# Value tiles for block A0 ahead of the dense part, and block B1's value rows summed on DVE

## The chip, the cores and the metric

The kernel runs on one core of a Trainium2 chip. The time is device microseconds of one execution; 2283.25 us is the median of three runs of the kernel before (2281.62 to 2299.92). Engines: PE multiplies matrices, DVE and POOL work on vectors, ACT on activations, and SP only issues transfers. POOL also issues the transfers whose addresses come from a list (indirect row fetches). Each engine takes its instructions in the order in which the program holds them.

## What is computed

One layer of a decoder for 512 prompt tokens and 8 sample tokens, 1024 wide, in f32. Differential attention and an mLSTM run in parallel and are merged; then comes the channel mixer, PEER, where the change lies:

```
q   = xn @ wq                         # 8 heads, two halves each
s   = q against 128 subkeys per half  # top 16 of each half, top 16 of the sums
eidx, g = 16 experts of 16384 per head, softmax of their scores
act = gelu(sum(xn * u[eidx]))         # 128 rows of peer_u per token
y   = x + sum((g * act) * v[eidx])    # 128 rows of peer_v per token
```

The prompt has two halves of 256 tokens, and each half two blocks of 128 tokens: A0 and A1 (first half), B0 and B1 (second half). The sample tokens go with the second half.

## The kernel before

For each block the scoring (`scores`, with its top-16 search) leaves 128 expert numbers and weights per token. `gather(hf, i)` then fetches, for each of the 128 columns, one row of `peer_u` per token: an indirect transfer of 512 KB (L1102, POOL) into one of six buffers of the pool `ring`, and a multiply with sum on DVE (L1108). `gelu_w` turns the sums S into weights.

The value side is computed in two ways. Blocks A0, A1 and B0 use a dense form: `w_block` spreads the weights of a block to a matrix W of 16384 experts by 128 tokens, in 32 groups of four tokens (one-hot tiles on DVE L1164, POOL L1167, DVE L1169 or L1177, ACT L145 and L1174, the products on PE L1181, copies L148), and `v_part` loads `peer_v` in 128 value tiles of 128x1024 f32 (512 KB each, L1275 on SP, five buffers) and multiplies each with the block's W (L1290, two matmuls of 512 columns per tile and block). Block B1 uses the other form, `vg_run`: 128 indirect transfers of one row of `peer_v` per expert slot of a token (L1313, POOL, twelve buffers called `vslab`) and a one-token matmul on each (L1318).

The tiles run as a ring: A0 and A1 take tiles 0 to 127 together, B0 joins at tile 100 (`JB`) and goes on alone through tiles 0 to 99; in that last piece B1's rows run beside it. W of a block occupies two slots of 64 tiles each; A0 and A1 hold two slots in each of two pools (`wr`, `wt`). W of A0 is built during the second half's scoring, W of A1 after it.

The order of the instructions on each engine is chosen by the framework's scheduler from its estimate of a time line, under the data and buffer dependencies of the program as written; on the chip it is fixed. A buffer of a pool is handed out in the program's order: whoever asks later for a buffer of `ring` waits until the one who had it before is done. `HOLD` delays the gather of a block until a step of the top-16 search.

Of the kernel before, what the change touches and what calls it, by code (L numbers as in the profile page):

```python
# [5 lines left out]
F32 = mybir.dt.float32  # L6
# [48 lines left out]
JH = 64  # L55
# [3 lines left out]
def step_kernel(  # L59
# [1051 lines left out]
    def gather(hf, i):  # L1111
        sel, todo = halves[hf]
        d, tok = sel[i], todo[i][0]
        if i == 0 and HOLD[hf] is not None:
            hb, hh = divmod(HOLD[hf], 8)
            with tc.issue_after(sel[hb]["last", hh][HE].ins):
                gather_dot(d, tok, OFF[i])
        else:
            gather_dot(d, tok, OFF[i])
        gelu_w(d["S"], d["g"], d["S"], d["top"], d["e"].bitcast(F32))  # L1120
# [63 lines left out]

    halves = []
    xx, early = project(0), None
    for hf in range(2):
# [58 lines left out]
        halves.append((scores(hf, todo, xx2), todo))  # L1246
        if hf == 0 and SV == 1:
# [24 lines left out]

    def v_part(j, use, split):
        vt = dp.tile([P, D], F32, tag="v", name="vtile", bufs=VB)
        nc.sync.dma_start(vt, v_rows[j * P:(j + 1) * P])  # L1275
        ws = [next(w[:, j - j0, :] for w, j0 in wT if j0 <= j < j0 + w.shape[1]) for _, wT, _, _ in use]
        pairs = [((w, vt),) for w in ws]
        if split:
            vh, vl = (ring.tile([P, D], F32R, tag="g", name=n) for n in ("vh", "vl"))
            wh, wl = (dp.tile([P, 2, P], F32R, tag="wh", name=n, bufs=3) for n in ("wh", "wl"))  # L1280
            copy(vh, vt)
            nc.vector.tensor_sub(vl, vt, vh.bitcast(F32))
            for b, w in enumerate(ws):
                copy(wh[:, b, :], w)
                nc.vector.tensor_sub(wl[:, b, :], w, wh[:, b, :].bitcast(F32))
            pairs = [((wh[:, b, :], vh), (wh[:, b, :], vl), (wl[:, b, :], vh)) for b in range(len(ws))]
        for (py, _, j0, j1), pp in zip(use, pairs):
            for i, (lw, rv) in enumerate(pp):
                for q in range(2):
                    nc.tensor.matmul(py[q], lw, rv[:, q * 512:(q + 1) * 512],  # L1290
                                     start=(j == j0 and i == 0), stop=(j == j1 and i == len(pp) - 1))

    def vg_prep(d, pool, wz):
        nc.gpsimd.memset(wz, 0.0)
        ef = pool.tile([P, P], F32, name="vg_ef", bufs=1)
        nc.vector.scalar_tensor_tensor(ef, d["i1"], 128.0, d["i2"], op0=ALU.mult, op1=ALU.add)
        p = pst_d()
        nc.tensor.transpose(p[:, 0:P], ef, ident)
        nc.tensor.transpose(p[:, P:2 * P], d["S"], ident)
        eT = pool.tile([P, P], I32, name="vg_eT", bufs=1)  # L1300
        nc.vector.tensor_copy(eT, p[:, 0:P])
        for j in range(4):
            copy(wz[:, j * 1024:(j + 1) * 1024:33], p[:, P + 32 * j:P + 32 * j + 32])
        return wz.rearrange("p (t c) -> p t c", c=32), eT

    def vg_run(prep, py, slots):
        wz, eT = prep
        for i in range(32):
            gts = []
            for j in range(4):  # L1310
                t = 32 * j + i
                gt = slots()
                nc.gpsimd.indirect_dma_start(out=gt, out_offset=None, in_=v_rows,  # L1313
                                             in_offset=bass.IndirectOffsetOnAxis(ap=eT[:, t:t + 1], axis=0))
                gts.append((j, t, gt))
            for q in range(2):
                for j, t, gt in gts:
                    nc.tensor.matmul(py[q][32 * j:32 * j + 32, :], wz[:, t, :], gt[:, q * 512:(q + 1) * 512],  # L1318
                                     start=(i == 0), stop=(i == 31), skip_group_check=True)
            yield  # L1320

    def v_done(tok, py):
        t = dp.tile([P, D], F32, tag="v", name="x1r", bufs=VB)
        nc.sync.dma_start(t, scr_x1[tok:tok + P])
        for q in range(2):
            nc.vector.tensor_add(t[:, q * 512:(q + 1) * 512], t[:, q * 512:(q + 1) * 512], py[q])  # L1326
        nc.sync.dma_start(y_prompt[0, tok:tok + P], t)
# [47 lines left out]
    useA = [(v_acc(0), wA0, 0, P - 1), (v_acc(1), wA1, 0, P - 1)]  # L1375
    for j in range(JH):
        v_part(j, useA, False)
    gather(1, 0)
# [3 lines left out]
    gather(1, 1)  # L1382
    wB0 = w_new(wr, wt)
    w_block(selB[0], wB0, wr, pst_d, 2)
    for j in range(JH, JB):
        v_part(j, useA, False)
    yB0 = v_acc(2)
    useB0 = (yB0, wB0, JB % P, (JB - 1) % P)
    for j in range(JB, P):
        v_part(j, useA + [useB0], False)  # L1390
    for b in range(2):
        v_done(b * P, useA[b][0])
    slab = [pool.tile([P, 8, D], F32, tag="WT", name="vslab", bufs=2) for pool in (wr, wt)]
    slot_i = [0]

    def slots():
        i = 4 + slot_i[0] % 12
        slot_i[0] += 1
        return slab[i // 8][:, i % 8, :]

    yB1 = v_acc(0)
# [46 lines left out]
```

## Time and profile before

| | |
|---|---|
| median of three runs | 2283.25 us (2281.62 to 2299.92) |
| the profiled execution | 2279.21 us, its span 2277.5 us |
| PE busy | 2098.4 us (92%) |
| DVE busy | 1403.7 us (62%) |
| POOL busy | 1327.5 us (58%) |
| ACT busy | 593.5 us (26%) |
| mean transfer rate | 303 GB/s, 690.15 MB |

The span runs from the first to the last instruction of the profiled execution. The scoring of the second half ends near 1301 us; the shared stream of A0 and A1 starts at 1351 and, with B0, holds PE to about 1930; from there B0 runs with B1's rows, and after 2194 B0 alone. A busy share is a mean over stages, so a reader takes the limit of each stage from the stretch itself.

### The profile page before, as it was taken

What the parts mean: (1) busy time and instruction counts of PE and PEld (TensorE: products, weight loads), DVE (VectorE), ACT (ScalarE), POOL (GpSimd) and SP (SyncE); (2) the same over time, 40 slices, a digit from 0 to 9 for tenths busy, and PEclk for the clock granted to TensorE, in tenths of its full rate; (3) what the DMA queues carried; (4) which work ended last, traced back from release to release, by engine and by line L of the source; (5) the groups of instructions that cost most, each with busy time, mean ns of one, the idle gap of its engine ahead of it and who ended that gap; (6) DMA issues with size and microseconds to landing.
All of it is one profiled execution on the core that took longest, in us unless ns stands there. A gap on an engine that the chain in (4) does not pass through costs nothing.

```text
span 2277.5 us, 26092 instructions
## 1 busy us (share of the span) xinstructions
PE 2098.4 (92%) x8208; PEld 1349.4 (59%) x8208; DVE 1403.7 (62%) x3382; ACT 593.5 (26%) x1615; POOL 1327.5 (58%) x1215
## 2 busy tenths in 40 slices
PE   6999899888999998998988866999999999899998
PEld 4776677777878776787766654444455544222233
DVE  1366675886799878767987989566388775000000
ACT  3334233312345323333423676000022100000000
POOL 0588773553586546667786778444278776555510
PEclk9999999989989999999998866999999999999999
DMA  5687676888799798999987147999699899999988
GB/s 161 198 269 236 229 239 229 282 297 287 243 329 324 269 321 321 337 369 313 318 311 245 43 167 248 410 409 409 252 365 355 320 403 362 410 407 409 409 332 284
DMA packets 293757, 690.15 MB, mean 303 GB/s; under 512 B 31054, under 2 KB 157066, under 8 KB 293618
## 3 DMA queue, kind: packets, MB, share of 16 engines
q0 software_dynamic: 112896, 411.09, 48.7%
q1 hardware_dynamic: 180722, 277.38, 35.1%
q8 instruction: 65, 1.06, 0.2%
q14 instruction: 74, 0.61, 0.1%
HBM read 670.19 MB, written 18.18 MB: 302 GB/s over the span
## 4 chain that ended last, share of the span: by engine, by line
PE 44%; DVE 11%; DMA 10%; issue 7%; POOL 5%; ACT 1%; DVEq 0%; POOLq 0%; ACTq 0%
PE y L1290 20%; PE ps_mm L288 9%; DMA vslab<-in_peer_v,vg_eT 6%; DVE urow L1108 3%; POOL urow L1102 3%; PE ps_mm L293 3%; PE y L1318 3%; PE ps_s L738 2%; DMA urow<-in_peer_u,k_e 1%; PE ps_w L1181 1%; POOL oh L1167 1%; PE ps_s L741 1%; DVE tk_w L975 1%; DVE ohe L1164 1%; DMA vpage<-in_cache_v,kidx 1%
## 5 line engine op out<-in xcount | busy, mean ns | idle before, releaser
L1102 POOL DMA_INDIRECT urow<-in_peer_u,k_e x512 | 632.2, 1235 | 326.9 <-DVE urow L1108 223.3
L1108 DVE SCALAR_TENSOR_TENSOR urow<-urow,xn 128x1024 f32<-128x1024 f32 x512 | 651.2, 1284 | 151.4 <-DMA urow<-in_peer_u,k_e 145.7
L1290 PE MATMUL y<-vtile,WT 128*128 128x512 f32 x1536 | 680.6, 598 | 3.0 <-DMA vtile<-in_peer_v 2.1
L1290 PEld LDWEIGHTS y<-vtile,WT 128*128 128x128 f32 x1536 | 286.6, 191 | 382.5 <-issue 377.8
L288 PE MATMUL ps_mm<-x,wch 128*128 128x264 f32 (+1 forms) x1536 | 385.9, 405 | 25.1 <-DVE sig L312 17.2
L288 PEld LDWEIGHTS ps_mm<-x,wch 128*128 128x128 f32 x1536 | 302.0, 201 | 81.5 <-DVE sig L312 20.7
L831 POOL TENSOR_TENSOR kpage<-kpage,qb 128x1024 f32<-128x1024 f32 x64 | 150.0, 2356 | 73.8 <-DMA qb<-scr_q 65.2
L288 PE MATMUL ps_mm<-hT,wch 128*128 128x256 f32 (+1 forms) x768 | 185.1, 391 | 0.7 <-DMA wch<-in_w_branch_b 0.5
L1313 POOL DMA_INDIRECT vslab<-in_peer_v,vg_eT x128 | 122.2, 955 | 106.2 <-DMA vslab<-in_peer_v,vg_eT 47.7
L1326 DVE TENSOR_TENSOR x1r<-x1r,y 128x512 f32<-128x512 f32 x8 | 5.2, 684 | 249.1 <-DMA x1r<-scr_x 238.3
L288 PEld LDWEIGHTS ps_mm<-hT,wch 128*128 128x128 f32 x768 | 144.4, 194 | 23.5 <-issue 1.3
L293 PE MATMUL ps_mm<-wch,x 128*128 128x256 f32 (+1 forms) x640 | 151.2, 388 | 0.3 <-DVE kS L690 0.3
L1318 PE MATMUL y<-vslab 128*32 128x512 f32 x512 | 138.6, 601 | 12.2 <-DMA vslab<-in_peer_v,vg_eT 12.2
L819 POOL DMA_INDIRECT vpage<-in_cache_v,kidx x64 | 79.8, 1248 | 106.6 <-DVE vacc L897 63.7
L1181 PE MATMUL ps_w<-oh,oh 128*128 128x128 f32 x512 | 88.3, 336 | 46.0 <-POOL oh L1167 29.2
L293 PEld LDWEIGHTS ps_mm<-wch,x 128*128 128x128 f32 (+1 forms) x640 | 108.3, 175 | 30.5 <-issue 2.8
L897 DVE SCALAR_TENSOR_TENSOR vacc<-vpage,aS,vacc 128x128 f32<-128x128 f32 x384 | 110.6, 359 | 19.4 <-DMA vpage<-in_cache_v,kidx 19.3
L1181 PEld LDWEIGHTS ps_w<-oh,oh 128*128 128x128 f32 x512 | 81.4, 242 | 62.3 <-POOL oh L1167 45.5
L1167 POOL TENSOR_TENSOR oh<-ohe,T_S 128x384 f32<-128x384 bf16 (+2 forms) x96 | 96.4, 1011 | 12.7 <-ACT T_S L148 5.6
L1318 PEld LDWEIGHTS y<-vslab 128*32 128x32 f32 x512 | 30.7, 109 | 112.0 <-issue 88.5
L832 DVE TENSOR_REDUCE sK<-kpage 128x16 f32<-128x1024 f32 x64 | 77.1, 1210 | 26.3 <-POOL kpage L831 26.2
L145 ACT ACTIVATE k_e<-k_top,zero 128x128 f32<-128x128 f32 x4 | 1.6, 402 | 346.0 <-DVE k_top L1126 346.0
(420 smaller groups left out, 2634.2 us busy)
## 6 DMA issues: line engine op xcount, KB each, us to landing
vtile<-in_peer_v SPq DMA_DIRECT2D x228, 512.0 KB
wch<-in_w_in SPq DMA_DIRECT2D x256, 256.0 KB
wch<-in_peer_wq SPq DMA_DIRECT2D x64, 256.0 KB
wch<-in_w_branch_a SPq DMA_DIRECT2D x32, 256.0 KB
wch<-in_w_branch_b SPq DMA_DIRECT2D x32, 256.0 KB
wch<-in_w_out SPq DMA_DIRECT2D x32, 256.0 KB
urow<-in_peer_u,k_e POOLq DMA_INDIRECT x512, 7.5
qb<-scr_q SPq DMA_DIRECT2D x8, 512.0 KB
```

What stands on the lines that cost most here:

```text
L288: nc.tensor.matmul(out, w[:, c0:c0 + m], xk[:, :n], start=(k == 0 and i == 0), stop=(k == KT - 1 and i == len(tt) - 1))
L293: nc.tensor.matmul(out, x[:, k, t0:t0 + m], ch[k // KP][:, k % KP, :n], start=(k == 0), stop=(k == KT - 1))
L819: nc.gpsimd.indirect_dma_start(out=t, out_offset=None, in_=rows, in_offset=bass.IndirectOffsetOnAxis(ap=kidx[:, b * 8 + pg:b * 8 + pg + 1] ...
L831: (nc.vector if KDV and pg % KDV == KDV - 1 else nc.gpsimd).tensor_mul(kt, kt, qb)
L897: nc.vector.scalar_tensor_tensor(acc[:, h, :], vt[:, h, :], wa, acc[:, h, :], op0=ALU.mult, op1=ALU.add)
L1102: nc.gpsimd.indirect_dma_start(out=gt, out_offset=None, in_=u_rows, in_offset=bass.IndirectOffsetOnAxis(ap=d["e"][:, k:k + 1], axis=0))
L1108: d["dot"] = nc.vector.scalar_tensor_tensor(gt, gt, 1.0, xn2, op0=ALU.mult, op1=ALU.mult, accum_out=d["S"][:, k:k + 1])
L1167: nc.gpsimd.tensor_mul(a[:, :PM], e.rearrange("p j t -> p t j")[:, :PM], sb[:, :PM])
L1181: nc.tensor.matmul(pw[:, t, :], b[:, t, :], a[:, t, :], start=True, stop=True)
L1290: nc.tensor.matmul(py[q], lw, rv[:, q * 512:(q + 1) * 512], start=(j == j0 and i == 0), stop=(j == j1 and i == len(pp) - 1))
L1313: nc.gpsimd.indirect_dma_start(out=gt, out_offset=None, in_=v_rows, in_offset=bass.IndirectOffsetOnAxis(ap=eT[:, t:t + 1], axis=0))
L1318: nc.tensor.matmul(py[q][32 * j:32 * j + 32, :], wz[:, t, :], gt[:, q * 512:(q + 1) * 512], start=(i == 0), stop=(i == 31), skip_group_che ...
```

## The change

`JC = 32` is new; the ring of tiles is cut into other pieces:

- During the second half, behind its scoring, `gather(1, 0)` (block B0's `peer_u` rows) is written first, and then A0 alone takes tiles 0 to 63 in buffers of `ring` (tag g), with accumulators in the projection's PSUM tiles; the sum is added to `scr_x1`.
- After that, A0 and A1 take tiles 64 to 127 together, and A0 ends; A1 takes tiles 0 to 31 alone and 32 to 63 with B0, and A1 ends; B0 goes on alone through 64 to 127 and 0 to 31.
- W of B0 goes to the two slots that A0 held, and `gelu_w` of B1 has a scratch tile of its own, since the expert numbers are needed later.
- B1's value rows are fetched per column (the same lists as for `peer_u`), into fifteen buffers made of A1's two slots, and each is multiplied by its weight and added to an accumulator on DVE (`v_rows_acc`); the accumulator starts from `scr_x1` and is stored as the block's output. `vg_prep` and `vg_run` go.

Value tiles: 228 before, 288 now. In the changed kernel, `v_part` loads on L1187 and multiplies on L1191; `v_done` loads, adds and stores on L1195, L1197, L1198; `v_rows_acc` loads on L1201, fetches on L1204, sums on L1206, stores on L1208.

```diff
--- before.py
+++ after.py
@@ -52,7 +52,7 @@
 BPE, NPE = (4, 4), (4, 2)
 EQD = (5, 6)
 EARLY = True
-JH = 64
+JH, JC = 64, 32
 SLOPES = [2.0 ** (-(h + 1)) for h in range(8)]
 
 
@@ -1108,7 +1108,7 @@
                 d["dot"] = nc.vector.scalar_tensor_tensor(gt, gt, 1.0, xn2, op0=ALU.mult, op1=ALU.mult,
                                                           accum_out=d["S"][:, k:k + 1])
 
-    def gather(hf, i):
+    def gather(hf, i, y=None):
         sel, todo = halves[hf]
         d, tok = sel[i], todo[i][0]
         if i == 0 and HOLD[hf] is not None:
@@ -1117,7 +1117,7 @@
                 gather_dot(d, tok, OFF[i])
         else:
             gather_dot(d, tok, OFF[i])
-        gelu_w(d["S"], d["g"], d["S"], d["top"], d["e"].bitcast(F32))
+        gelu_w(d["S"], d["g"], d["S"], d["top"], d["e"].bitcast(F32) if y is None else y())
 
     def gelu_w(s, g, out, t, y):
         nc.vector.tensor_mul(t, s, s)
@@ -1182,6 +1182,31 @@
             for w, j0 in wT:
                 copy(w[:, :, t0:t0 + TG], pw[:, :, j0:j0 + w.shape[1]].rearrange("p t j -> p j t"))
 
+    def v_part(j, use, slot):
+        vt = slot()
+        nc.sync.dma_start(vt, v_rows[j * P:(j + 1) * P])
+        for py, wT, j0, j1 in use:
+            w = next(w[:, j - b, :] for w, b in wT if b <= j < b + w.shape[1])
+            for q in range(2):
+                nc.tensor.matmul(py[q], w, vt[:, q * 512:(q + 1) * 512], start=(j == j0), stop=(j == j1))
+
+    def v_done(slot, tok, py, dst):
+        t = slot()
+        nc.sync.dma_start(t, scr_x1[tok:tok + P])
+        for q in range(2):
+            nc.vector.tensor_add(t[:, q * 512:(q + 1) * 512], t[:, q * 512:(q + 1) * 512], py[q])
+        nc.sync.dma_start(dst[tok:tok + P], t)
+
+    def v_rows_acc(d, tok, acc, slot):
+        nc.sync.dma_start(acc, scr_x1[tok:tok + P])
+        for k in range(P):
+            gt = slot()
+            nc.gpsimd.indirect_dma_start(out=gt, out_offset=None, in_=v_rows,
+                                         in_offset=bass.IndirectOffsetOnAxis(ap=d["e"][:, k:k + 1], axis=0))
+            nc.vector.scalar_tensor_tensor(acc, gt, d["S"][:, k:k + 1], acc, op0=ALU.mult, op1=ALU.add)
+            yield
+        nc.sync.dma_start(y_prompt[0, tok:tok + P], acc)
+
     halves = []
     xx, early = project(0), None
     for hf in range(2):
@@ -1244,6 +1269,12 @@
             else:
                 w_block(halves[0][0][0], wA0, wr, pst_w, 0)
         halves.append((scores(hf, todo, xx2), todo))
+        if hf == 1:
+            gather(1, 0)
+            yA0 = [pst("a"), pst("o")]
+            for j in range(JH):
+                v_part(j, [(yA0, wA0, 0, JH - 1)], lambda: sgt([P, D], "vtile"))
+            v_done(lambda: sgt([P, D], "x1r"), 0, yA0, scr_x1)
         if hf == 0 and SV == 1:
             with tc.high_priority() if HPV else ExitStack():
                 sample_values(aS)
@@ -1269,62 +1300,6 @@
 
     def v_acc(b):
         return [dps.tile([P, 512], F32, tag=f"y{b}{q}", name=f"y{b}{q}") for q in range(2)]
-
-    def v_part(j, use, split):
...
-        for (py, _, j0, j1), pp in zip(use, pairs):
-            for i, (lw, rv) in enumerate(pp):
-                for q in range(2):
-                    nc.tensor.matmul(py[q], lw, rv[:, q * 512:(q + 1) * 512],
-                                     start=(j == j0 and i == 0), stop=(j == j1 and i == len(pp) - 1))
-
-    def vg_prep(d, pool, wz):
...
-    def vg_run(prep, py, slots):
...
-    def v_done(tok, py):
...
     def sample_peer():
         s64 = ring.tile([64, 2, P], F32, tag="g", name="s64")
@@ -1372,46 +1347,43 @@
             nc.vector.tensor_add(x1s[:, q * 512:(q + 1) * 512], x1s[:, q * 512:(q + 1) * 512], py[q][:NS, :])
...
-    useA = [(v_acc(0), wA0, 0, P - 1), (v_acc(1), wA1, 0, P - 1)]
-    for j in range(JH):
-        v_part(j, useA, False)
-    gather(1, 0)
+    def vslot():
+        return dp.tile([P, D], F32, tag="v", name="vtile", bufs=VB)
+
+    useA0 = (v_acc(0), wA0, JH, P - 1)
+    useA1 = (v_acc(1), wA1, JH, JH - 1)
+    for j in range(JH, P):
+        v_part(j, [useA0, useA1], vslot)
+    v_done(vslot, 0, useA0[0], y_prompt[0])
     steps = sample_peer()
     for _ in range(SST[0]):
         next(steps)
-    gather(1, 1)
-    wB0 = w_new(wr, wt)
+    gather(1, 1, lambda: wr.tile([P, P], F32, name="ge_y", bufs=1))
+    wB0 = w_new(wr, wr)
     w_block(selB[0], wB0, wr, pst_d, 2)
-    for j in range(JH, JB):
-        v_part(j, useA, False)
-    yB0 = v_acc(2)
-    useB0 = (yB0, wB0, JB % P, (JB - 1) % P)
-    for j in range(JB, P):
-        v_part(j, useA + [useB0], False)
-    for b in range(2):
-        v_done(b * P, useA[b][0])
-    slab = [pool.tile([P, 8, D], F32, tag="WT", name="vslab", bufs=2) for pool in (wr, wt)]
+    useB0 = (v_acc(2), wB0, JC, JC - 1)
+    for j in range(JH):
+        v_part(j, [useA1] + ([useB0] if j >= JC else []), vslot)
+    v_done(vslot, P, useA1[0], y_prompt[0])
+    slab = [wt.tile([P, 8, D], F32, tag="WT", name="vslab", bufs=2) for _ in range(2)]
     slot_i = [0]
 
-    def slots():
-        i = 4 + slot_i[0] % 12
+    def gslot():
+        i = slot_i[0] % 15 + 1
         slot_i[0] += 1
         return slab[i // 8][:, i % 8, :]
 
-    yB1 = v_acc(0)
-    run = vg_run(vg_prep(selB[1], dp, slab[0][:, 0:4, :].rearrange("p a c -> p (a c)")), yB1, slots)
-    for j in range(JB):
-        v_part(j, [useB0], False)
-        if j % 3 == 2:
-            next(run, None)
-        if j >= SST[1] and j % SST[2] == 0:
+    run = v_rows_acc(selB[1], HALF + P, slab[0][:, 0, :], gslot)
+    for i, j in enumerate([*range(JH, P), *range(JC)]):
+        v_part(j, [useB0], vslot)
+        next(run, None)
+        if i % SST[2] == 0:
             next(steps, None)
-    v_done(HALF, yB0)
+    v_done(vslot, HALF, useB0[0], y_prompt[0])
     for _ in run:
-        pass
+        next(steps, None)
     for _ in steps:
         pass
-    v_done(HALF + P, yB1)
     dctx.close()
     ctx.close()
```

Three places in the order of the instructions follow.

SP, the loads behind the second half's scoring: before, loads of value tiles, which wait for PE and for other transfers (`DMAHW`, and `DMASW` those that POOL issues).

```order
601 L1275 DMA vtile<-in_peer_v 128x1024 [waits DMAHW6_49,PE_49]
602 L1275 DMA vtile<-in_peer_v 128x1024 [waits DMAHW7_49,PE_49]
603 L1275 DMA vtile<-in_peer_v 128x1024 [waits DMAHW0_49,PE_49]
604 L1275 DMA vtile<-in_peer_v 128x1024 [waits DMAHW1_49,PE_49]
605 L1275 DMA vtile<-in_peer_v 128x1024 [waits DMAHW2_49,PE_49]
```

The same place in the changed kernel (rows 597 to 601 are five loads into the dense part's own buffers, those for tiles 64 to 68; from row 602 on the loads go to buffers of `ring`, tiles 0, 1, ...).

```order
600 L1187 DMA vtile<-in_peer_v 128x1024 [waits DMAHW1_49]
601 L1187 DMA vtile<-in_peer_v 128x1024 [waits DMAHW2_49]
602 L1187 DMA vtile<-in_peer_v 128x1024 [waits DMASW4_49,DMASW5_49,DMASW3_49,DMASW6_49,DMASW2_49,DMASW7_49,DMASW1_49,DMAHW3_49,DMASW0_49,DVE_49]
603 L1187 DMA vtile<-in_peer_v 128x1024 [waits DMASW6_49,DMAHW4_49,DMASW1_49,DVE_49]
604 L1187 DMA vtile<-in_peer_v 128x1024 [waits DMASW6_49,DMASW4_49,DMAHW5_49,DMASW1_49,DVE_49]
605 L1187 DMA vtile<-in_peer_v 128x1024 [waits DMAHW6_49,DMASW6_49,DVE_49]
606 L1187 DMA vtile<-in_peer_v 128x1024 [waits DMASW7_49,DMASW3_49,DMAHW7_49,DMASW0_49,DVE_49]
607 L1187 DMA vtile<-in_peer_v 128x1024 [waits DMAHW0_49,DVE_49]
608 L1099 DMA xn_12073<-scr_xn_59 128x1024 [waits DMAHW1_49]
609 L1187 DMA vtile<-in_peer_v 128x1024 [waits DMAHW3_49,DMAHW2_49,PE_49]
```

Six loads now wait for DVE, each for one of the last six dots of `gather(1, 0)`, whose buffers they take; the load of the next block's `xn`, into the one buffer that those dots read, stands behind them.

POOL, the same time: the rows of `gather(1, 0)` (L1102) and the build of W for A1 (L1167). Before:

```order
461 L1102 DMA urow<-in_peer_u,k_e 128x1024 x5
462 L1013 TENSOR_TENSOR tk_eq<-tk_eq,tk_sf 128x512
463 L1167 TENSOR_TENSOR oh_10578<-ohe,T_S 128x256
464 L1167 TENSOR_TENSOR oh_10596<-ohe,T_S 128x256
465 L1102 DMA urow<-in_peer_u,k_e 128x1024 x4
466 L1167 TENSOR_TENSOR oh_10614<-ohe,T_S 128x256
467 L1102 DMA urow<-in_peer_u,k_e 128x1024
468 L1167 TENSOR_TENSOR oh_10632<-ohe,T_S 128x256
```

In the changed kernel (the L989 to L1013 rows of 64 partitions are the sample tokens' top-16 search):

```order
450 L1102 DMA urow<-in_peer_u,k_e 128x1024 x5
451 L1013 TENSOR_TENSOR tk_eq<-tk_eq,tk_sf 128x512
452 L1102 DMA urow<-in_peer_u,k_e 128x1024 x123
453 L989 TENSOR_TENSOR tk_c<-tk_sv 64x120
...
461 L1102 DMA urow<-in_peer_u,k_e 128x1024 x3
462 L1167 TENSOR_TENSOR oh_11040<-ohe,T_S 128x256
463 L1167 TENSOR_TENSOR oh_11058<-ohe,T_S 128x256
464 L1102 DMA urow<-in_peer_u,k_e 128x1024 x2
465 L1167 TENSOR_TENSOR oh_11076<-ohe,T_S 128x256
466 L1102 DMA urow<-in_peer_u,k_e 128x1024
```

All 128 rows of `gather(1, 0)` now stand ahead of the first step of A1's W; between the 32 groups of that W stand 52 rows of the next block's gather (`gather(1, 1)`) instead. On PE, A0's 128 matmuls (L1191) stand between the last scoring matmul and the first transpose of A1's W, and behind that only five of the dense part's A0 tiles stand ahead of the 32 groups.

SP, the end of the program. Before:

```order
310 L1275 DMA vtile<-in_peer_v 128x1024 x5
311 L1373 DMA out_y_sample<-x1s 8x1024
312 L1275 DMA vtile<-in_peer_v 128x1024 x77
313 L1324 DMA x1r<-scr_x_58 128x1024 x2
314 L1327 DMA out_y_prompt<-x1r 128x1024 x2
```

In the changed kernel:

```order
319 L1348 DMA out_y_sample<-x1s 8x1024
320 L1187 DMA vtile<-in_peer_v 128x1024 x35
321 L1208 DMA out_y_prompt<-vslab 128x1024
322 L1187 DMA vtile<-in_peer_v 128x1024 x49
323 L1195 DMA vtile<-scr_x_58 128x1024
324 L1198 DMA out_y_prompt<-vtile 128x1024
```

The store of B1's sums (row 321) stands ahead of the last 49 value tiles in SP's queue.

## Rows read from the trace of the kernel before

**Rows 1.** The page, its head and the engines' busy time

```profile
span 2277.5 us, 26092 instructions
...
PE 2098.4 (92%) x8208; PEld 1349.4 (59%) x8208; DVE 1403.7 (62%) x3382; ACT 593.5 (26%) x1615; POOL 1327.5 (58%) x1215
```

**Rows 2.** Busy time, count by engine; then PE's clock, transfer share and rate

```profile
core 0: us, PE busy (x) PEld busy (x) DVE busy (x) ACT busy (x) POOL busy (x), PEclk, DMA share, GB/s
...
1250.00:1300.00 50.00, 45.32 (x225) 36.38 (x223) 49.76 (x299) 27.12 (x73) 37.10 (x74) 0.97 0.19 60
...
1300.00:1350.00 50.00, 26.70 (x112) 22.82 (x111) 45.10 (x164) 38.45 (x118) 34.60 (x51) 0.53 0.21 71
...
1450.00:1500.00 50.00, 50.00 (x118) 22.15 (x117) 30.73 (x50) 0.00 (x0) 22.58 (x25) 1.00 1.03 409
...
2200.00:2250.00 50.00, 50.00 (x118) 22.18 (x117) 0.00 (x0) 0.00 (x0) 0.00 (x0) 1.00 0.87 304
```

**Rows 3.** The chain of waits: start, length, and what held the end

```profile
1350.89 5.89 PE y L1290 x8
...
1425.53 232.88 PE y L1290 x542
...
2194.04 72.31 PE y L1290 x168
...
2266.37 4.50 DMA x1r<-scr_x
```

**Rows 4.** The page's costliest groups: dots on DVE, one-token matmuls on PE

```profile
L1108 DVE SCALAR_TENSOR_TENSOR urow<-urow,xn 128x1024 f32<-128x1024 f32 x512 | 651.2, 1284 | 151.4 <-DMA urow<-in_peer_u,k_e 145.7
...
L1318 PE MATMUL y<-vslab 128*32 128x512 f32 x512 | 138.6, 601 | 12.2 <-DMA vslab<-in_peer_v,vg_eT 12.2
```

**Rows 5.** The time line of PE behind the scoring: start, length, instruction

```profile
1301.48 0.69 PE L1141 MATMUL ps_w<-ident,k_i 128*128 128x128 f32 x2 [0.46 <-ACT sss L148]
...
1308.56 0.77 PE L1181 MATMUL ps_w<-oh,oh 128*128 128x128 f32 x2 [5.77 <-ACT oh L1174]
```

**Rows 6.** The time lines of POOL and DVE: the gather's first row, first dot

```profile
1336.77 1.56 POOL L1102 DMA_INDIRECT urow<-in_peer_u,k_e  x1 [0.15 <-issue]
...
1341.57 1.23 DVE L1108 SCALAR_TENSOR_TENSOR urow<-urow,xn 128x1024 f32<-128x1024 f32 x1 [2.82 <-DMA urow<-in_peer_u,k_e]
```

**Rows 7.** Busy time and count, 1304 to 1337: L1167, L1164, L1169 in turn

```profile
1304.00:1337.00 33.00, 7.16 (x11) 0.55 0.00 1
...
1304.00:1337.00 33.00, 6.58 (x14) 0.55 0.00 1
...
1304.00:1337.00 33.00, 5.17 (x11) 0.55 0.00 1
```

**Rows 8.** Busy time of POOL on L1102 alone, two stretches

```profile
1346.00:1415.00 69.00, 36.81 (x32) 0.65 0.79 273
...
1825.00:1900.00 75.00, 60.66 (x45) 1.00 1.02 403
```

**Rows 9.** The time line of POOL: one row fetch while DVE sums

```profile
1830.59 1.63 POOL L1102 DMA_INDIRECT urow<-in_peer_u,k_e  x1 [0.30 <-issue]
```

**Rows 10.** Busy time of PE on L1181 alone: W of A1, then of B0

```profile
1346.00:1415.00 69.00, 35.55 (x168) 0.65 0.79 273
...
1668.00:1784.00 116.00, 27.27 (x224) 1.00 0.98 363
```

**Rows 11.** ACT's groups, 1346 to 1415: busy, mean ns, idle before

```profile
L145 ACT ACTIVATE oh<-iota,T_n 128x128 f32<-128x128 f32 x72 | 23.0, 398 | 0.0
L148 ACT ACTIVATE WT<-ps_w 128x256 f32<-128x256 f32 x40 | 13.1, 380 | 21.5 <-PE ps_w L1181 21.4
L1174 ACT ACTIVATE oh<-oh,one 128x512 f32<-128x512 f32 x18 | 12.6, 717 | 0.1
```

**Rows 12.** Busy time, 1950 to 2150: POOL on L1313, PE on L1290

```profile
1950.00:2150.00 200.00, 95.11 (x100) 1.00 1.03 409
...
1950.00:2150.00 200.00, 81.33 (x164) 1.00 1.03 409
```

More of the change, by code (lines that the diff above doesn't have):

```diff
@@ L1271, in v_acc @@
         return [dps.tile([P, 512], F32, tag=f"y{b}{q}", name=f"y{b}{q}") for q in range(2)]
-    def v_part(j, use, split):
[L1274 to L1286, printed above, removed]
-        for (py, _, j0, j1), pp in zip(use, pairs):
-            for i, (lw, rv) in enumerate(pp):
-                for q in range(2):
-                    nc.tensor.matmul(py[q], lw, rv[:, q * 512:(q + 1) * 512],
-                                     start=(j == j0 and i == 0), stop=(j == j1 and i == len(pp) - 1))
@@ L1293, in vg_prep @@
-    def vg_prep(d, pool, wz):
[L1294 to L1304, printed above, removed]
@@ L1306, in vg_run @@
-    def vg_run(prep, py, slots):
[L1307 to L1320, printed above, removed]
@@ L1322, in v_done @@
-    def v_done(tok, py):
[L1323 to L1327, printed above, removed]
     def sample_peer():
```

## The prediction

> **What bounds the kernel now.** I read the page first, then the busy time in stretches, then the chain of waits, and last the rows of single lines. PE is busy 92% of a span of 2277.5 us [rows 1], but the limits differ by stage. While the second half is scored (1250 to 1300 us) DVE is busy 49.8 of 50 us and the DMA engines move 60 GB/s; from 1300 to 1350 PE is down to 26.7 of 50 us; from 1425 on PE is full and the DMA engines move up to 409 GB/s [rows 2]. The chain says the same: 232.88 us for 542 matmuls of L1290 in one piece [rows 3], so 0.430 us a record and, at four records to a value tile and block (each of the two 512-column matmuls stands as two records), **1.72 us per tile and block**. The last piece, 168 matmuls in 72.31 us, is 42 tiles of one block at 1.72 us: there PE is the limit at 304 GB/s [rows 2, 3]. At 409 GB/s a piece of 512 KB takes 0.524 MB / 409 = **1.282 us**; that is the floor of a row fetch or a tile load when transfers queue up.
>
> The idle part is therefore the 120 us around 1300 to 1415, and the change wants to put A0's first 64 tiles there. Whether it can is a question of order. The A0 tiles take their buffers from the ring that `gather(1, 0)` uses, behind it, and the order on SP shows the sixth to eleventh load of a tile waiting for DVE: they wait for the last dots of that gather. The five loads ahead of them are for the later dense part. So PE does nothing of this stream between the end of scoring and the end of `gather(1, 0)`, and that gather, which lay beside PE's stream before, now stands alone on the path. On PE the whole of A1's W follows A0's 64 tiles, while before it filled the same hole as the gather's start. I cost the changed program stage by stage from there.
>
> **Start of the gather.** POOL issues the first row of the second half at 1336.77 [rows 6]. Ahead of that, from 1304 to 1337, POOL spent 7.16 us and DVE 6.58 + 5.17 = 11.75 us on A1's W [rows 7], which is later now. DVE is the engine on which the retrieval hangs [rows 2], so I take 12 us off: 1325 (bounds 1318 and 1337).
>
> **`gather(1, 0)` alone.** 128 rows. From 1346 to 1415, with dots beside, 32 issues took 36.81 us [rows 8], 1.15 us each, and between issues lie 0.30 us [rows 9]: a pitch of 1.45 us. Lower bound: 0.95 us an issue where DVE sums nothing [rows 12] plus 0.30 is 1.25, and the DMA floor is 1.282, so 164 us. Upper: 60.66 us for 45 issues over 75 us [rows 8], 1.67 us, 214 us. Value tiles filled the DMA engines in that stretch, here they don't, so I take 1.45: 186 us, and 5 us from the last issue to its dot (1336.77 to 1341.57) [rows 6]. That is **1516**.
>
> One rule speaks against that number. The row's evidence stands above: an issue is 1.15 us with dots beside it and 0.95 us without. The Trainium skill, "SBUF — State Buffer", section Who interferes with whom, says that a DVE instruction with two SBUF inputs contends with a GpSimd instruction that reads SBUF, and that the one that comes second is blocked for the whole of the first. By that rule the pitch of an issue and a dot would be 0.95 + 0.30 + 1.28 = 2.53 us and this term 324 us. The trace agrees in direction only, with 0.20 us of 1.28, and the measured pitch stands.
>
> **A0's 64 tiles.** 64 x 1.72 = 110 us, and 2.5 us for a start at the lower clock: after the hole eight matmuls took 5.89 us [rows 3] for 3.43, at a granted clock of 0.53 in that stretch [rows 2]. **1628.5**. SP's x1r load, the two adds and the sample tokens' top-k come behind them, beside the next stage's start.
>
> **W of A1, with PE nearly empty.** Before, 7 us lay between the transposes and the first W matmul [rows 5]; with the two adds I take 9 us. From 1346 to 1415 stand 168 records of L1181 [rows 10]; a group has four matmuls and so eight records, which makes 21 groups: 69 / 21 = 3.29 us a group, beside 32 / 21 = 1.52 gather rows each. In the new order POOL has 52 rows of `gather(1, 1)` between the 32 groups, 1.63 each, so 3.29 + 0.11 x 1.45 = 3.45 us and 110 us in all. Lower bound: ACT's work of that stretch, 23.0 + 13.1 + 12.6 = 48.7 us [rows 11] for 19 groups, 2.56 us a group, 82 us. Upper: rows at 1.63 + 0.30 = 1.93 us [rows 9] and 0.97 us of POOL's own multiply, 1.63 x 1.93 + 0.97 = 4.1, 131 us. Before, part of this was covered by the A stream; now only 5 tiles of A0 lie beside it. **1747.5**.
>
> **A0 and A1 together, tiles 64 to 127.** 128 tile-blocks less those 5: 123 x 1.72 = 212 us, and 2.5 us again for the low clock: **1962**. The other 67 rows of `gather(1, 1)`, the 16 sample rows and 64 tiles need 147 x 1.282 = 188 us of DMA: covered.
>
> **A1's tiles 0 to 63 with B0's 32 to 63.** 96 x 1.72 = 165 us. 30 of the 32 W groups of B0 lie on PE between these: 27.27 us for 224 records, 28 groups, is 0.97 each [rows 10], 29 us. B0's first tile needs all 32 groups: at ACT's 2.56 us a group [rows 11] they take 82 us, and A1's 32 tiles alone with those 29 us last 84; at 3.29 us they would take 105, a wait of 21. POOL's first seven `vslab` rows of B1 stand ahead of those W steps and wait for A1's second-half matmuls to end. For both I add 10 us (bounds: nothing and 25): 204 us, **2166**.
>
> **The tail.** B0 alone has 96 tiles, B1 128 rows of which 7 are summed and 14 fetched at its start. On SP the store of the sums stands ahead of the last 49 tiles, and it waits for all 128 sums. So 42 tiles and 107 rows go first: 149 x 1.282 = 191 us. The stretch from 1950 to 2150 is the same mix: 100 rows and 164 matmuls, 41 tiles, in 200 us at 409 GB/s [rows 12]. A sum on DVE (1.28 us by the dot's row [rows 4]) is hidden under a row's 1.78 us. Then store, first landing and 49 tiles at PE's pace: 7 + 49 x 1.72 = 91 us. **2448**. Bounds: 107 rows at 1.67 = 179 us below; 107 at 2.0 = 214 us above.
>
> **End.** The last matmul was at 2266.35, 11 us before the end [rows 1, 3]; the same load, add and store stand there: span 2459. The profiled execution takes 1.7 us more than its span (2279.2), so **2460 us**, 181 more than the profiled execution. That one is 4 us under the median of 2283.25, well inside the spread of the runs shown (18 us).
>
> **Where it goes.** 228 value tiles become 288 (60 x 1.72 = 103 us of PE more), the one-token matmuls leave PE (138.6 us [rows 4]), so PE has 35 us less to do; the loss is the stretches in which PE waits: 190 us for the gather, 119 for W, some 110 in the tail.
>
> **Rivals.** (A) *The tiles do run beside scoring and gather.* Then DMA would bound from 1325 on: 288 tiles, 384 rows, 16 sample rows and 8 broadcasts, 696 x 1.282 = 892 us, span 1325 + 892 + 11 = 2228 and time 2230, 2.2% faster. For it: 60 to 71 GB/s and a half-idle PE between 1250 and 1350 [rows 2]. Against: the order on SP, from which nothing can escape since each engine keeps its order. It decides if the first A0 matmul stands before 1400. Chance 0.06. (B) *Sums block the issue of rows.* If an issue (0.95 us), the gap (0.30) and a sum (1.28) [rows 4, 9, 12] followed one another, the pitch would be 2.53 us and the tail's 107 rows would take 271 instead of 191 us: 2540. For it: 1.15 against 0.95 us; against: only 0.20 us lost per issue. It decides at a pitch above 1.78 us in the tail. Chance 0.07. (The Trainium skill's rule above, at its full price, would be this rival.) (C) *Milder.* Rows at their floor (-22 us), W at ACT's pace (-28), rows ahead of tiles (-12), no start for B0 (-10) and more W hidden by A0: 2330 to 2385, chance 0.05. (D) *Losses cancel*, within 1%: 0.03.
>
> **Numbers.** My own case has 0.79. Its range: the lower bounds together take 22 + 28 + 10 + 12 = 72 us off, 2388; the upper ones add 28 + 21 + 15 + 23 = 87, 2547. That all of one side come together is unlikely, so the start's own 7 and 12 us are not added. Rival B falls inside. 2385 to 2545 leaves out A, C and D, 0.14 together. A measurement tells 1%, 23 us, from no change: faster 0.06, same 0.03, slower 0.91.
>
> **What would show it.** PE empty from about 1305 to 1516 while L1102 runs at 1.45 us a row; the first L1191 near 1516; L1181 every 3.4 us from 1640 to 1750 with PE mostly idle; the last 49 tiles at 304 GB/s behind the store of L1208. Wrong if L1191 starts before 1400, if W of A1 lies beside a full stream, or if the store's place costs the last tiles nothing.

## The result and the profile after

The changed kernel takes 2517.7 us (median of four runs, 2507 to 2536) against 2282.4 us: a ratio of 1.1016, 95% interval 1.095 to 1.108. The prediction was 2460 us, between 2385 and 2545. The profiled execution took 2535.8 us.

The page's head, PE's line of its first part and three groups of the fifth, to set beside [rows 1, 4] (form: line, engine, operation, count | busy us, mean ns | idle before, and what ended it):

```profile
span 2534.1 us, 25417 instructions
...
PE 1998.9 (79%) x7694; PEld 1338.9 (53%) x7694; DVE 1570.9 (62%) x3508; ACT 597.9 (24%) x1611; POOL 1351.8 (53%) x1214
...
L1204 POOL DMA_INDIRECT vslab<-in_peer_v,k_e x128 | 148.2, 1158 | 224.5 <-PE y L1191 147.6
L1191 PE MATMUL ps_a<-vtile,WT 128*128 128x512 f32 x128 | 66.4, 601 | 220.8 <-DMA vtile<-in_peer_v 220.8
L1206 DVE SCALAR_TENSOR_TENSOR vslab<-vslab,k_S 128x1024 f32<-128x1024 f32 x128 | 166.9, 1304 | 58.6 <-DMA vslab<-in_peer_v,k_e 55.7
```

PE has 100 us less to do and the span is 257 us longer: PE waits. One wait of 220.8 us stands ahead of A0's first matmul. The page calls its end a landing of a value tile, which is only the last link; why the tile came so late is told by SP's waits (who waits <- for whom: us in total, times, longest):

```profile
SPq L1187 <- DVE urow L1108: 185.7, 5, 180.2
SPq L1208 <- DVE vslab L1206: 96.2, 1, 96.2
```

The first row is the load of a tile that stands still 180 us for a dot of `gather(1, 0)`; the second is the store of B1's sums, with 49 tiles behind it. The DMA engines were not free during the first wait. While the gather's 128 rows were issued, they moved 356 GB/s (POOL on L1102: length of the stretch, busy time and count, PE's clock, transfer share and rate):

```profile
1351.00:1549.00 198.00, 145.00 (x128) 0.50 0.96 356
```

Busy time by stretch shows what both cost (columns as in [rows 2]):

```profile
1300.00:1350.00 50.00, 23.39 (x115) 18.21 (x113) 49.90 (x278) 20.22 (x57) 35.81 (x69) 0.74 0.01 2
...
1450.00:1500.00 50.00, 0.00 (x0) 0.00 (x0) 43.17 (x70) 0.00 (x0) 39.33 (x36) 0.50 0.98 365
...
1600.00:1650.00 50.00, 50.00 (x118) 22.21 (x117) 0.00 (x0) 0.00 (x0) 0.00 (x0) 1.00 0.88 306
...
1700.00:1750.00 50.00, 26.33 (x106) 22.41 (x106) 43.26 (x71) 32.04 (x93) 44.88 (x37) 0.53 0.73 232
...
2350.00:2400.00 50.00, 3.97 (x8) 1.35 (x8) 47.32 (x37) 0.00 (x0) 36.43 (x35) 0.58 1.03 409
...
2450.00:2500.00 50.00, 50.00 (x118) 22.18 (x117) 0.00 (x0) 0.00 (x0) 0.00 (x0) 1.00 0.88 302
```

Read them as the prediction's stages: the end of scoring, with almost no transfers; PE at nothing while rows come in; A0 alone, PE full, DVE, ACT and POOL at nothing; W of A1 with POOL at 45 of 50 us and PE half used at the lower clock; rows and sums with PE at 4 of 50 us; the last tiles at PE's pace. Each engine is idle in turn.

### The profile page after: what moved, and what is told of

It reads as the page before. It is cut to its first block, busy times and chain, and to the rows that moved or that the text cites. A ratio compares the mean times of both kernels' runs of the same rounds, so it can differ in the third digit from the quotient of the medians.

```text
span 2534.1 us, 25417 instructions
## 1 busy us (share of the span) xinstructions
PE 1998.9 (79%) x7694; PEld 1338.9 (53%) x7694; DVE 1570.9 (62%) x3508; ACT 597.9 (24%) x1611; POOL 1351.8 (53%) x1214
## 5 line engine op out<-in xcount | busy, mean ns | idle before, releaser
L1102 POOL DMA_INDIRECT urow<-in_peer_u,k_e x512 | 629.5, 1230 | 285.1 <-DVE urow L1108 166.9
L1108 DVE SCALAR_TENSOR_TENSOR urow<-urow,xn 128x1024 f32<-128x1024 f32 x512 | 643.6, 1266 | 131.6 <-DMA urow<-in_peer_u,k_e 123.5
L1191 PE MATMUL y<-vtile,WT 128*128 128x512 f32 x1280 | 568.3, 598 | 110.4 <-DMA vtile<-in_peer_v 109.9
L1191 PEld LDWEIGHTS y<-vtile,WT 128*128 128x128 f32 x1280 | 238.9, 191 | 423.0 <-issue 281.2
L1204 POOL DMA_INDIRECT vslab<-in_peer_v,k_e x128 | 148.2, 1158 | 224.5 <-PE y L1191 147.6
L1191 PE MATMUL ps_a<-vtile,WT 128*128 128x512 f32 x128 | 66.4, 601 | 220.8 <-DMA vtile<-in_peer_v 220.8
L1206 DVE SCALAR_TENSOR_TENSOR vslab<-vslab,k_S 128x1024 f32<-128x1024 f32 x128 | 166.9, 1304 | 58.6 <-DMA vslab<-in_peer_v,k_e 55.7
L1191 PEld LDWEIGHTS ps_a<-vtile,WT 128*128 128x128 f32 x128 | 24.6, 193 | 251.9 <-DMA vtile<-in_peer_v 221.3
L1181 PE MATMUL ps_w<-oh,oh 128*128 128x128 f32 x512 | 99.7, 359 | 73.1 <-POOL oh L1167 69.0
L1197 DVE TENSOR_TENSOR vtile<-vtile,y 128x512 f32<-128x512 f32 x6 | 4.1, 687 | 239.3 <-PE y L1191 239.3
L1181 PEld LDWEIGHTS ps_w<-oh,oh 128*128 128x128 f32 x512 | 88.7, 259 | 94.9 <-POOL oh L1167 87.1
L1167 POOL TENSOR_TENSOR oh<-ohe,T_S 128x384 f32<-128x384 bf16 (+2 forms) x96 | 106.3, 1114 | 27.1 <-PE ps_w L1181 17.6
L989 POOL TENSOR_TENSOR tk_c<-tk_sv 128x120 f32<-128x120 f32 (+1 forms) x33 | 18.5, 560 | 189.6 <-DVE tk_sv L976 169.7
```

Of the source, the lines that this page charges most:

```text
L1102: nc.gpsimd.indirect_dma_start(out=gt, out_offset=None, in_=u_rows, in_offset=bass.IndirectOffsetOnAxis(ap=d["e"][:, k:k + 1], axis=0))
L1108: d["dot"] = nc.vector.scalar_tensor_tensor(gt, gt, 1.0, xn2, op0=ALU.mult, op1=ALU.mult, accum_out=d["S"][:, k:k + 1])
L1167: nc.gpsimd.tensor_mul(a[:, :PM], e.rearrange("p j t -> p t j")[:, :PM], sb[:, :PM])
L1181: nc.tensor.matmul(pw[:, t, :], b[:, t, :], a[:, t, :], start=True, stop=True)
L1191: nc.tensor.matmul(py[q], w, vt[:, q * 512:(q + 1) * 512], start=(j == j0), stop=(j == j1))
L1206: nc.vector.scalar_tensor_tensor(acc, gt, d["S"][:, k:k + 1], acc, op0=ALU.mult, op1=ALU.add)
```

## The experiments

Ratios are to the kernel before, with 95% intervals. Each is to runs of the kernel before taken with it, whose medians lay between 2282 and 2290 us, so a difference in us between two kernels that were not timed together is uncertain by some 8 us. No edit stands for `again`: it is the changed kernel.

**The changed kernel once more.** 

> The changed kernel once more, unchanged, as the base for the others. Its profiled execution lay 18 us above the median of its runs, and its scoring ended at 1327.7 us against 1300.6 before, on instructions that stand in the same order in both kernels up to there. If those 27 us belong to the one execution, scoring ends between 1300 and 1315 here and the profiled time lies between 2505 and 2520; if they belong to the change (another layout of its buffers, say), scoring ends at 1325 or later again, in every profile of this form.

2512.6 us, 1.0977 (1.0907 to 1.1046). Scoring ended at 1304.9 us, so the 27 us belonged to the one execution; the profiled time, 2524.3, was still above the range given for it.

**The store on another queue.**

```diff
-        nc.sync.dma_start(y_prompt[0, tok:tok + P], acc)
+        nc.scalar.dma_start(y_prompt[0, tok:tok + P], acc)
```

> One edit: the store of the summed rows is issued by ACT's queue, so that the last 49 value tiles no longer stand behind it on SP; nothing else moves. Theory (the store's place empties the tail): 91 tiles and 107 rows then share the DMA engines from the end of A1 on, 198 x 1.282 = 254 us, against 215 + 91 = 306 measured in the changed kernel: about 2470 us, 45 less, with the DMA engines at 409 GB/s to the end and PE never empty for 80 us. Rival 1 (the sums on DVE set the pace of the tail): the tiles fit beside the rows, the tail lasts the 215 us that the rows take, 90 less, about 2428. Rival 2 (the tiles would have waited for the DMA engines anyhow): no change, 2518.

2512.7 us, 1.099 (1.092 to 1.106): no change, though for another reason than rival 2's. SP's waits in this kernel's tail:

```profile
SPq L1187 <- PE y L1191: 144.2, 85, 4.2
SPq L1187 <- DMA out_y_prompt<-vslab: 87.9, 1, 87.9
```

A tile load on SP waited 88 us for the store on ACT. The program makes the direct transfers of both queues take turns on eight completion semaphores (`DMAHW0` to `DMAHW7` in its waits), and the load that is next on the store's semaphore waits for the store.

**The store on POOL.** The same line with `nc.gpsimd`. 

> The changed kernel with one edit: the store of the summed rows is issued by POOL, behind its last row fetch. Moving it to ACT's queue gained nothing, as a load on SP still waited 88 us for that store: the direct transfers of all queues take turns on eight completion semaphores, and the load that came eighth after the store had to wait for it. POOL's transfers count on semaphores of their own. Theory (the tail is 306 us because the last 49 tiles wait for the store): 91 tiles and 107 rows share the DMA engines, 198 x 1.282 = 254 us, about 2465 us (2455 to 2480), and no load on SP waits for the store. Rival (the tail is bound by rows and sums whatever the tiles do): the rows then slow down as the tiles come in and the end stays, 2500 to 2515.

2491.4 us, 1.0884 (1.081 to 1.096): 21 us less than the changed kernel in its second timing, half of the 45 expected, in the gap between both ranges. The interval overlaps that of `again` slightly, so the traces decide what happened. Three stretches of the tail:

```profile
2250.00:2300.00 50.00, 38.23 (x79) 13.16 (x78) 29.09 (x23) 0.00 (x0) 29.19 (x20) 1.00 1.03 409
2300.00:2350.00 50.00, 38.56 (x79) 12.90 (x77) 25.25 (x20) 0.00 (x0) 27.37 (x21) 1.00 1.03 409
2350.00:2400.00 50.00, 38.96 (x79) 13.54 (x80) 24.83 (x20) 0.00 (x0) 27.44 (x20) 1.00 1.03 410
```

The DMA engines are full and PE is busy in each stretch, as the theory wanted, and no load waits for the store any more. From A1's last add to the end are 284 us (2200 to 2484) where the changed kernel's second profile has 311 (2211 to 2523). The 254 us of transfers were counted too low. The DMA engines moved 112.38 MB in those 284 us, which is 214 pieces of 512 KB instead of 198 (114 rows, 93 tile loads, three stores, the load of `x1r` and the sample tokens' rows): 275 us at 1.282. The other 9 lie at the two ends of the stretch, where the rate is lower.

**A0's tiles ahead of the gather.**

```diff
-            gather(1, 0)
             yA0 = [pst("a"), pst("o")]
...
             v_done(lambda: sgt([P, D], "x1r"), 0, yA0, scr_x1)
+            gather(1, 0)
```

> One edit: A0's 64 tiles are written ahead of the gather of B0's rows instead of behind it, so that they no longer wait for its last dots; the gather's rows then lie beside the build of W of A1 and the shared stream, and the next block's rows move further back. Theory (PE idle during the gather, 197 us and 24 us of waiting for its start, is the main loss): A0's matmuls start where scoring ends, W of A1 is done some 220 us earlier, and from there the DMA engines bound the rest: about 335 rows, 219 tiles and 8 broadcasts, 562 x 1.282 = 720 us; 2290 to 2340 us in all. Rival 1 (the gather's time is merely moved, since PE stands still again where its rows are needed): above 2450. Rival 2 (60 more tiles and sums on DVE are the loss, not the wait): 2480 or more.

2382.5 us, 1.0405 (1.032 to 1.049): 130 us less. A0's first matmul stands 8 us behind the scoring and has lost the wait:

```profile
1325.85 2.08 PE L1191 MATMUL ps_a<-vtile,WT 128*128 128x512 f32 x2 [7.99 <-DMA vtile<-in_peer_v]
```

W of A1 is done 264 us behind the end of scoring (1317.4 to 1580.9) instead of 478 (1304.9 to 1783.0 in the changed kernel's second profile), 215 us earlier, as expected. The median is 42 us above the upper end of the expected range. Of the 215 us, 85 are given back: the gather's rows now lie beside the streams, the DMA engines move 395 to 410 GB/s from 1900 to 2300, and PE waits 122 us for tiles from 1640 on, 64 of them behind the store, which still stands ahead of the last tiles.

**Half of the gather's rows.** B0's `peer_u` rows 64 to 127 are left out, and that half of S is copied from the first.

```diff
-        for k in range(P):
+        for k in range(n):
...
+        if n < P:
+            nc.vector.tensor_copy(d["S"][:, n:], d["S"][:, :P - n])
```

> The changed kernel with half of one gather left out: of B0's 128 rows of peer_u only 64 are fetched and summed, and the other half of S is a copy of the first. Everything else stands as it was, so this prices the term of the gather by itself. Theory (the gather stands alone on the path, A0's tiles behind it): 64 rows at the measured pitch of 200 / 128 = 1.56 us less, 95 to 100 us, about 2415 us, with A0's first matmul 100 us nearer to the end of the scoring. Rival (PE would stand still at that place anyway, for the tiles' landing, the W of A1 or the top-16 search): less than 30 us.

2405.0 us, 1.052 (1.042 to 1.062): 108 us less. A0's first matmul comes 128 us behind the scoring (1307.0 to 1434.7) instead of 224 (1304.9 to 1528.9), so 96 of them are the gather's, 1.50 us a row; where the other 12 came from is not settled. PE's wait there (L1194 is the tiles' matmul in this kernel; the changed kernel has 220.8):

```profile
PE ps_a L1194 <- DMA vtile<-in_peer_v: 127.2, 1, 127.2
```

This is the gather's price with nothing moved.

**B1's gather behind W of A1.**

```diff
+    d = selB[1]
+    nc.vector.scalar_tensor_tensor(d["top"], wA1[0][0][:, 0, :], 0.0, d["i2"], op0=ALU.mult, op1=ALU.add)
+    nc.vector.scalar_tensor_tensor(d["e"], d["i1"], 128.0, d["top"], op0=ALU.mult, op1=ALU.add)
     gather(1, 1, lambda: wr.tile([P, P], F32, name="ge_y", bufs=1))
```

> One edit: the expert numbers of block B1 are computed once more on DVE (two instructions of 128x128) from a column of the finished W of A1 times zero, so that the gather of B1 cannot start before W of A1 is done; its 61 rows leave the build of that W. Theory (POOL's turns between rows and W steps stretch the build to 163 us): the build takes 9 us of lead and 32 groups at 2.6 to 3.1 us, 92 to 110 us, and the rows find room beside the following 400 us of PE-bound stream: 55 to 70 us less, about 2455 us. Rival 1 (ACT, DVE or PE sets the pace of the build whatever POOL does): no change, 2518. Rival 2 (the rows come back in the tail, as the DMA engines have no room earlier): the build shrinks by 55 us and the tail grows by as much, 2510 to 2520.

2495.5 us, 1.093 (1.086 to 1.100); against the changed kernel's second timing 17 us less, not clear of its interval. The mechanism is clear in the trace: from A0's last early matmul to the next shared one are 88 us (1634 to 1723) instead of 141 (1642 to 1783). What PE's W matmuls waited for in that build, in the changed kernel's second profile and here (us, times), and the first shared matmul here:

```profile
  POOL oh L1167: 70.2, 31
...
  ACT oh L1174: 21.1, 21
  POOL oh L1167: 1.3, 1
...
1722.95 8.85 PE L1191 MATMUL y<-vtile,WT 128*128 128x512 f32 x20 [0.64 <-ACT WT L148]
```

ACT now sets the pace, 2.23 us a group (1650.8 to 1722.2 for 32). The 2.56 us that the prediction took from ACT's rows as a lower bound were therefore too many: it added the busy times of three lines, which overlap (from 1651 to 1722 they add up to 78.3 us here, and ACT is busy 68.5 of 71). The rows come back not in the tail but beside W of B0: that stage, A0's end to A1's, holds 36 of them and grew from 207 us (2004 to 2211) to 248 (1934 to 2182). PE now waits there 21 us for POOL, 8 before, and 11.5 us for tiles, none before. Of 53 us, 41 are given back: rival 2's outcome, at another place.

**The sums alone, in the kernel before.**

```diff
-    run = vg_run(vg_prep(selB[1], dp, slab[0][:, 0:4, :].rearrange("p a c -> p (a c)")), yB1, slots)
+    run = v_rows_acc(selB[1], HALF + P, slab[0][:, 0, :], slots)
```

The new gather scratch tile and slot numbers are those of the change; in the loop over B0's tiles four rows go with three tiles, as before.

> The kernel before with one part of the change alone: block B1's value rows are fetched per column and summed on DVE (fifteen buffers), and the one-token matmuls go; ring of tiles, gathers and W stay as before. Theory (a sum of 1.3 us is hidden under a row at 1.8 us): the rows end about where they ended, at 2180 to 2195, and behind the store, which stands ahead of the last 53 tiles on SP, come 53 x 1.72 + 7 = 98 us: about 2290 us, within 1% of before. Rival (each sum blocks the issue of a row, pitch 0.95 + 0.30 + 1.28 = 2.53 us): the rows end at 1930 + 324 = 2254 and the end comes at about 2360.

2295.9 us, 1.002 (0.999 to 1.005): the same. The sums are not what costs.

**The sums alone, the store on POOL.** 

> The same part alone, and the store of the sums issued by POOL, so that no value tile stands behind it. Theory: the DMA engines are then full to the end; the 42 tiles that lie at PE's pace behind the rows in the kernel before (72 us) take 42 x 1.282 = 54 us: about 2265 us, 0.8% under before. Rival (sums block the issue of rows): 2330 or more.

2271.2 us, 0.994 (0.9905 to 0.9975), ten runs: the one version that beats both kernels, by 0.6% over the kernel before. At the end its DMA engines hold 409 GB/s where the kernel before falls to 304 [rows 2]:

```profile
2100.00:2150.00 50.00, 38.51 (x79) 13.23 (x79) 24.90 (x20) 0.00 (x0) 27.46 (x20) 1.00 1.03 409
2150.00:2200.00 50.00, 38.64 (x80) 13.19 (x78) 25.41 (x20) 0.00 (x0) 27.15 (x20) 1.00 1.03 409
2200.00:2250.00 50.00, 42.05 (x90) 15.67 (x89) 18.26 (x15) 0.00 (x0) 10.25 (x8) 1.00 0.99 384
```

**Both repairs of the changed kernel.** Tiles ahead of the gather, store on POOL. 

> Both repairs of the changed kernel together: A0's tiles written ahead of the gather, and the store issued by POOL. Measured with the first alone: 2382 us, and there 33 tiles stand behind the store, 64 us at PE's pace; they would take 42 us or less beside the rows, and the 7 us of the store and the first landing go: about 2350 us (2335 to 2365). What then remains over the kernel before, some 65 us, would be the 60 more value tiles, 60 x 1.282 = 77 us of transfers in stretches where the DMA engines are full. Rival (the repairs overlap, the tail being bound elsewhere): 2375 or more.

2366.4 us, 1.032 (1.026 to 1.038): 16 us less than the first alone, half of what was expected (and the intervals overlap), and 79 us above the kernel before.

**One resident tile for 32, twice.** The loads of A1's tiles 0 to 31 are left out, with both repairs in.

```diff
+    vt0 = ring.tile([P, D], F32, tag="g", name="vtile0")
+    nc.sync.dma_start(vt0, v_rows[0:P])
     for j in range(JH):
-        v_part(j, [useA1] + ([useB0] if j >= JC else []), vslot)
+        v_part(j, [useA1] + ([useB0] if j >= JC else []), vslot, vt0 if j < JC else None)
```

> The kernel with both repairs, and 31 loads left out: in the stage in which A1 runs alone, tiles 0 to 31, one resident tile stands in for all 32 (the matmuls remain). Theory (what remains over the kernel before is the transfers of 60 more tiles): 31 x 1.282 = 40 us less, 2366 - 40 = 2326 us (2315 to 2345), since the DMA engines are at 400 GB/s or more in nearly all stretches from 1600 on. Rival (that stage is bound by PE and W of B0, and the tail by the rows' own chain of fetch and sum): 2355 or more.

2432.9 us, 1.062 (1.052 to 1.072): 66 us more with 31 transfers less. The tile had been put in the ring:

```profile
SPq L1367 <- DVE urow L1108: 189.8, 1, 189.8
```

That is the changed kernel's wait in another place: whoever asks for a buffer of the ring behind a gather waits for the gather. With `vt0 = vslot()` instead: 

> The same question as the run before, with the resident tile in one of the dense part's own five buffers. In the run before it sat in the ring, behind the gather of B1, and its load waited 190 us for that gather's dots: the wait that this study is about, made once more by mistake, so that the run says nothing of the transfers. Left out here as there: 31 loads of A1's tiles 0 to 31, one tile standing in. Theory (what remains over the kernel before is the transfers of 60 more tiles): 40 us less than with both repairs, 2366 - 40 = 2326 us (2315 to 2345). Rival (that stage is bound by PE, the tail by fetch and sum): 2355 or more.

2341.4 us, 1.024 (1.019 to 1.030): 25 us less, or 19 by the ratios, whose intervals overlap; that is 0.6 to 0.8 us a load. The transfers of 60 more tiles are then some 36 to 48 of the 79 us that remain, an estimate from that rate, which one stage gave; the rest is not settled. In the kernel with both repairs PE waits from 1600 on 20 us for W steps and 30 us for the sample tokens' rows and products, where the kernel before has 1 and none. Neither was tried. The second can't be taken as a price by itself, for the sums alone with the store on POOL, the fastest version, has 51 us of it.

## Why the prediction was right, step by step

The direction and the places were right: the wait of the tiles on the ring, W of A1 in the open, the store ahead of 49 tiles. `swap` and `halfrows` show the first, `wlate` the second, `pool` the third, each by less than its length (130, 17 and 21 us of the total). Stage lengths, in us, from the profiled execution of the changed kernel:

| stage | forecast | measured |
|---|---|---|
| scoring's end | 1301 | 1328 |
| to the gather's first row | 24 | 24 |
| gather, to A0's first matmul | 191 | 197 |
| A0's 64 tiles | 112 | 111 |
| W of A1 | 119 | 138 |
| A0 with A1 | 214 | 220 |
| A1 with B0 | 204 | 205 |
| rows and 42 tiles, to the store | 191 | 215 |
| last 49 tiles | 91 | 91 |
| the rest | 11 | 4 |

Rows of the time lines from which three of them are taken: the gather's first row, A0's first matmul, the tiles' matmuls ahead of A1's W, its first and last matmuls and the next of the shared stream.

```profile
1351.58 1.04 POOL L1102 DMA_INDIRECT urow<-in_peer_u,k_e  x1
...
1548.89 2.07 PE L1191 MATMUL ps_a<-vtile,WT 128*128 128x512 f32 x2 [220.82 <-DMA vtile<-in_peer_v]
...
1663.40 8.75 PE L1191 MATMUL y<-vtile,WT 128*128 128x512 f32 x20
...
1682.20 3.59 PE L1181 MATMUL ps_w<-oh,oh 128*128 128x128 f32 x16 [9.95 <-POOL oh L1167]
...
1794.31 2.93 PE L1181 MATMUL ps_w<-oh,oh 128*128 128x128 f32 x12 [2.87 <-POOL oh L1167]
...
1797.98 2.46 PE L1191 MATMUL y<-vtile,WT 128*128 128x512 f32 x5 [0.38 <-ACT WT L148]
```

Of the 75 us by which the span exceeded the forecast, 27 lie ahead of any instruction that the change moved. The stages behind them are no accident of one execution: in the second profile each is within 3 us of these. Three terms were mis-sized; the gather and the shared stream are 6 us longer each. The misses of W of A1 and of the tail's rows fell on the same side, both at the upper bounds that the prediction gave them (138 us against 140, 215 against 214).

- **W of A1, 19 us.** The pace held (1682 to 1797 for 32 groups, 3.6 us each against 3.45). The lead did not, 22 us (1660 to 1682) against 9. The matmuls of the five tiles, 8.8 us, stand between the first transposes and the last, and not beside the W. Behind them PE waits 10 us for POOL's first W step: nine rows of `gather(1, 1)` stand ahead of it, 13.2 us of issue between 1663 and 1681, and the prediction counted only the rows between the groups. They could be read in the order. In `wlate`, without these rows, PE's wait is 1.3 us, and the lead still 17.
- **The rows of the tail, 24 us.** Taken were 107 rows, 21 having been fetched early. From 2224 to 2438 POOL issued 115:

```profile
2224.00:2352.00 128.00, 73.97 (x57) 0.99 1.02 404
2352.00:2438.00 86.00, 58.61 (x58) 0.53 0.97 385
```

  (POOL on L1204: length of the stretch, busy time and count, PE's clock, transfer share and rate.) POOL had waited 147.6 us for A1's matmuls to free the slots. The DMA engines moved 84.73 MB from 2224 to 2438, 162 pieces of 512 KB where the term had 149: eight rows, two tile loads, a store and the sample tokens' rows more, 16 us at the floor of 1.282. The remaining 8 lie at the two ends of the stretch (344 GB/s in its first 10 us, 119 in its last 6), for which the term had nothing.
- **The end, 7 us less.** The last matmul's end and the span's end are 4 us apart here, where the load of `x1r` had been put behind the last matmul before.

Two readings of the prediction that moved no stage were wrong. The 60 tiles more are loads, not work for PE: both kernels have 1536 records of the tiles' matmuls, so PE has 100 us less to do and not 35. And PE was half idle only from 1300 to 1350, not from 1250 [rows 2].

On the rivals. (A) falls: no A0 matmul before 1548. (B) falls, though not by the sign that the prediction named, a pitch above 1.78 us in the tail: over both rows above the pitch is 1.86, but in the first the transfers are at 404 GB/s with tiles beside the rows, which explains it without B. The second row is 1.48 us a row with a sum on DVE beside each, far from 2.53, and `rowsum` is no slower than before. The rule that the prediction took for B, of the Trainium skill, "SBUF — State Buffer", section Who interferes with whom, is for a GpSimd instruction that reads SBUF. The same section infers that making a transfer's descriptors needs the write interface, of which a DVE `tensor_tensor` takes nothing. The sums here are a `scalar_tensor_tensor`, also with two inputs, and the 1.48 us agree with that; no run here shows which interface an issue uses. For POOL's multiplies, which read SBUF as the rule wants, the trace leans its way: a W multiply beside dots took 1.52 us in several places of the changed kernel (0.75 in others):

```profile
1714.31 1.52 POOL L1167 TENSOR_TENSOR oh<-ohe,T_S 128x256 f32<-128x256 bf16 x1
```

The 32 multiplies of that build average 1.15 us, and 0.81 in `wlate`, where neither dots nor row issues lie beside them. No experiment here separated the two. (C) and (D) did not come; the pitch was above the forecast, not at the floor.

What the prediction said of the store's cost was half right. It is the cause of the empty PE, but removing it returned 21 us of an 88 us wait, the longest of PE's for a tile there (in all, times, longest):

```profile
PE y L1191 <- DMA vtile<-in_peer_v: 109.5, 36, 88.2
```

In `pool` the tail is bound by the DMA engines, at 409 GB/s from 2250 to 2450: the tiles that move into the gap slow the rows.

## What to carry to other kernels

A buffer pool is a queue: work written behind a gather in the same pool starts when the gather ends, however idle its engine is. Beside the gather there was little room for tiles here (356 GB/s); what helped was to write them ahead of it, so that its rows lie beside later work. Look at what a load waits for, not at what the engine waits for, and price a repair at the next limit, since of 215, 53 and 88 us by which three repairs brought PE's work forward, 130, 17 and 21 reached the end. Before blaming a queue's order, see whether its transfers share completion semaphores with another's.

## What the runs showed of the hardware

The stretch up to the end of scoring has the same instructions in the same order in all twelve kernels, but its length ranged from 1300.6 to 1327.7 us over the profiles (1304.9 and 1327.7 for the same kernel). In the longest, PE's granted clock fell to 0.69 between 200 and 250 us, with the transfer rate at 155 GB/s against 232 before. Why is open. A difference of 20 us between two single profiles of this kernel says nothing until the stage that differs has been found.
